# First loads of a decoder trunk: finer pieces of x, the norm vectors in x's rows, one weight buffer kept aside at the start

## The chip, the core and the metric

The kernel runs on one core of a Trainium2 chip. The metric is the device time of one execution in microseconds (us). TensorE (PE in the rows, PEld for its weight loads), VectorE (DVE), ScalarE (ACT), GpSimd (POOL) and SyncE (SP) run their own instruction streams and wait for each other by semaphores. Transfers between device memory and the on-chip memory are issued by SP (SPq in the rows), ACT (ACTq) or POOL, and run on the core's 16 DMA engines.

## What is computed

One decoder layer over 256 tokens of width 2048, all in float32: a token mixer with three groups of attention heads, a cross attention over 256 memory vectors, and a gated feed-forward block of width 5632, each with a residual add.

```
h = rms_norm(x, g_mix)
qa, ka, va, qb, kb, vb, qc, kc, vc = split(h @ w_in)
x = x + concat(diff_attention, moba_attention, dilated_attention) @ w_out
x = x + memory_cross_attention(rms_norm(x, g_cross), rms_norm(mem, g_mem), w_cq, w_ckv, w_co)
x = x + conv_glu_ffn(rms_norm(x, g_ffn), w_up, conv_w, conv_b, w_down)
out = rms_norm(x, g_final)
```

Each weight is read once.

## The kernel before

**Pieces and halves.** All weights are cut into pieces of 1 MB (128 partitions of 2048 floats), in the order in which they are used. A piece has two halves of 512 KB. Below, p0, p1, ... are the pieces and half 0, half 1, ... the halves, so half i is part i % 2 of piece i // 2. Each half goes through the same steps: it is loaded into a raw buffer; ACT copies it, rounded, into a tile `hi` (L141); DVE subtracts `hi` from it into a tile `lo` (L148); then PE multiplies (L296 with `hi`, L303 with `lo`). In the first chunk of `w_in` a half is 8 products with `hi` and 8 with `lo`. A raw buffer is free again once the `lo` tiles of both its halves are made.

**Buffers.** There are `NRAW = 4` raw buffers and `NSPLIT = 5` pairs of `hi` and `lo`. A piece's load waits until a raw buffer is free; a piece takes the buffer that the program frees first. `load` (L116) issues a whole piece from SP as one transfer, `load_half` (L130) half of one, `load_block` (L926) a quarter.

**x.** The input x lies transposed as 16 blocks of 128 channels by 256 tokens (`xT`, 2 MB in all). `high` (L194, on ACT) and `low` (L197, on DVE) multiply a block by its norm gain, a column of the tile `gT`, and write two parts of it into `hT`, which PE reads. Half i (for i up to 7) needs blocks 2i and 2i + 1. `put_x` does two blocks.

**Order.** There is no scheduler: each engine runs its instructions in the order in which this program writes them. The main loop (L1015) goes over the halves. In step i the `hi` copy and the `lo` subtraction of half i + `LEAD` (4 ahead) are written before half i's products; functions put down with `before(i, ...)` stand ahead of the `lo` of that step and those with `after(i, ...)` behind the products. Halves 2 to 7 are split by `after(i, ...)` of steps 0 to 5 instead, together with `put_x` (L973). Thus half 8 is split at the head of step 4, ahead of half 6, which is split at its end. At the head of step 4 the loads of p4, p5 and p6 are written on SP as well, p7 in step 6. The sums of squares of x (`square_part`, L215) and the norm factors (`norm_factors`, L230) are put down for steps 5 to 13: `fold` on DVE in step 10 and two small products on PE (`total`, L242) behind half 10.

**Loads.** SP issues its loads in order. Loads issued by SP and ACT take eight counters in turn (DMAHW0 to DMAHW7 in the rows below), so a load also waits until the load eight places earlier, which used its counter, has landed. The first loads stand at L933 to L944; p3 follows at L971. The norm gains, the first counter's load, are issued by ACT at L171 as an array of their own.

Of the kernel before, what the change touches and what calls it, by code (L numbers as in the profile page):

```python
# [11 lines left out]
F32 = mybir.dt.float32  # L12
# [5 lines left out]
P = 128  # L18
D = 2048
S = 256  # L20
NT = 2
KD = D // P
# [12 lines left out]
HALF = 1024  # L35
NRAW = 4
NSPLIT = 5
LEAD = 4
NACC = 5
MIX, MEM, CROSS, FFN = range(4)  # L40


BUCKET_AT = list(range(17)) + [22, 30, 40, 54, 73, 99, 134, 182, 246]
# [15 lines left out]


@with_exitstack
def trunk(ctx, tc, x, mem, gains, w_in, w_out, diff_lambda, rel_bias_table, w_cq, w_ckv, w_co, w_up, conv, w_down,
          g_final, onehot, biasadd, out):
    nc = tc.nc
    PE, DVE, ACT, POOL, SP = nc.tensor, nc.vector, nc.scalar, nc.gpsimd, nc.sync
    PSUM = bass.MemoryType.PSUM

    cst = ctx.enter_context(tc.tile_pool(name="cst", bufs=1))
    wpool = ctx.enter_context(tc.tile_pool(name="wpool", bufs=1))
# [23 lines left out]
    def small(n, name, bufs=4):  # L93
        return tmp.tile([P, n], F32, tag=f"sm_{name}", name=name, bufs=bufs)
# [10 lines left out]
    pieces = []  # L105
# [6 lines left out]
    def new_raw(p):  # L112
        if p.raw is None:
            p.raw = wpool.tile([P, 2 * HALF], F32, tag="raw", name="raw", bufs=NRAW)
# [15 lines left out]
    def load_half(p, h):  # L130
        new_raw(p)
        src = p.srcs[0]
        k = src.ap[1][1] // 2
        half = bass.AP(tensor=src.tensor, offset=src.offset + h * k * src.ap[1][0],
                       ap=[list(src.ap[0]), [src.ap[1][0], k], list(src.ap[2])])
        SP.dma_start(p.raw[:, h * HALF:(h + 1) * HALF].rearrange("p (k n) -> p k n", k=k), half)
# [20 lines left out]
    def before(i, f):  # L157
        pre.setdefault(i, []).append(f)
# [8 lines left out]

    gT = cst.tile([P, 4 * KD + 1], F32, name="gT")  # L170
    ACT.dma_start(gT, gains)  # L171
    subg = gT[:, 4 * KD:]
    mhalf = cst.tile([P, 1], F32, name="mhalf")
    POOL.memset(mhalf, -0.5)
    ones = cst.tile([P, 1], F32, name="ones")
    POOL.memset(ones, 1.0)
    ident = cst.tile([P, P], F32, name="ident")
    make_identity(nc, ident)
    ACT.copy(small(1, "first", 1), mhalf)


    xT = cst.tile([P, KD, S], F32, name="xT")


    def rstd_of(ss, n, width, r=None):
# [724 lines left out]
    for k in range(KF):  # L910
        src = bass.AP(tensor=w_down.tensor, offset=w_down.offset + k * P * D, ap=[[D, P], [1, D]])
# [9 lines left out]


    def load_x(a, n):
        SP.dma_start(xT[:, a:a + n, :], x[:, a:a + n, :])

    def load_block(p, k):  # L926
        new_raw(p)
        src = p.srcs[0]
        SP.dma_start(p.raw[:, k * 512:(k + 1) * 512],
                     bass.AP(tensor=src.tensor, offset=src.offset + k * src.ap[1][0],  # L930
                             ap=[list(src.ap[0]), list(src.ap[2])]))

    load_x(0, 2)  # L933
    load_block(pieces[0], 0)
    load_block(pieces[0], 1)
    load_x(2, 2)
    load_half(pieces[0], 1)
    load_x(4, 4)
    load_half(pieces[1], 0)
    load_half(pieces[1], 1)  # L940
    load_x(8, 4)
    load_half(pieces[2], 0)
    load_half(pieces[2], 1)
    load_x(12, 4)  # L944


    warm = acc_tile()
# [15 lines left out]
    p = pieces[0]  # L963
    p.parts[0] = hi, lo = [wpool.tile([P, HALF], F32R, tag=t, name=t, bufs=NSPLIT) for t in ("hi", "lo")]
    for j in range(2):
        c = slice(j * 512, (j + 1) * 512)
# [69 lines left out]
def packed(a):  # L1036

    return a.reshape(-1, P, a.shape[-1]).transpose(1, 0, 2)
# [24 lines left out]
```

## Time and profile before

| | |
|---|---|
| median of 3 runs | 1261.15 us (1261.11 to 1261.88) |
| profiled execution, its own time | 1260.96 us |
| its span, first to last instruction | 1259.2 us |
| PE busy | 1243.1 us (99%) |
| PE weight loads busy | 1078.2 us (86%) |
| DVE busy | 831.4 us (66%) |
| ACT busy | 630.3 us (50%) |
| bytes moved | 233.23 MB, mean 185 GB/s |

The profiled execution took 1.8 us more than its span. Busy time is an average over the whole span; the change touches the first loads, so the table says little of it, and the stretches at the start have to be read one by one.

### The profile page before, as it was taken

Reading aid. Unit: us, or ns where it says so; the run is one execution under the profiler, and the core shown is the slowest. Engines: PE = TensorE matmul, PEld = TensorE weight load, DVE = VectorE, ACT = ScalarE, POOL = GpSimd, SP = SyncE. Lnnn points to the kernel's source line nnn. Section 1 sums busy time; section 2 is a strip of 40 time slices with the busy share of each in tenths; the row PEclk is TensorE's granted clock in tenths of the full one; section 3 lists DMA queues with packets and bytes.
Section 4 is the critical chain, followed back from the end, with each engine's and each line's share of the span. In section 5 each row is a group of like instructions: output and inputs, shape, how many; then the busy total and the mean of one; then the engine's idle time right before and its main releaser. Section 6 shows DMA issues by size and latency. Waiting matters only on the chain.

```text
span 1259.2 us, 17608 instructions
## 1 busy us (share of the span) xinstructions
PE 1243.1 (99%) x6928; PEld 1078.2 (86%) x6928; DVE 831.4 (66%) x1350; ACT 630.3 (50%) x979; POOL 12.2 (1%) x22
## 2 busy tenths in 40 slices
PE   7999999999999999999999999999999999999997
PEld 6888888988888899888888888888888888888885
DVE  5755677566568877776667768767676754544555
ACT  6545555556455656545444444444444544444444
POOL 0000000000000000000000000000000000000000
PEclk9999999999999999999999999999999999999999
DMA  8755554554566544565565565555656555555541
GB/s 301 236 176 188 186 167 162 181 183 159 174 223 215 170 167 162 202 203 171 167 200 182 186 197 174 183 199 184 198 170 201 186 183 200 181 187 200 175 160 67
DMA packets 104835, 233.23 MB, mean 185 GB/s; under 512 B 4336, under 2 KB 14896, under 8 KB 98992
## 3 DMA queue, kind: packets, MB, share of 16 engines
q1 hardware_dynamic: 104576, 232.05, 55.2%
q8 instruction: 54, 0.88, 0.3%
q14 instruction: 29, 0.24, 0.1%
q10 hardware_dynamic: 144, 0.03, 0.0%
q0 software_dynamic: 32, 0.02, 0.0%
HBM read 229.97 MB, written 2.12 MB: 184 GB/s over the span
## 4 chain that ended last, share of the span: by engine, by line
issue 58%; PE 39%; DMA 2%; DVE 0%; POOL 0%; ACT 0%; SPq 0%; DVEq 0%; POOLq 0%; ACTq 0%
PE acc L296 16%; PE acc L303 9%; PE acc L342 3%; PE acc L344 3%; PE acc L343 3%; DMA raw<-in_w_in 2%; PE at L402 1%; PE acc L299 1%; PE acc L298 1%; PE at L421 0%; PE at L445 0%; PE at L473 0%; PE at L474 0%; ACT hi L141 0%; POOL raw L866 0%
## 5 line engine op out<-in xcount | busy, mean ns | idle before, releaser
L148 DVE TENSOR_TENSOR lo<-raw,hi 128x1024 fp32r<-128x1024 f32 x423 | 517.1, 1223 | 368.1 <-ACT hi L141 367.5
L141 ACT CAST hi<-raw 128x1024 fp32r<-128x1024 f32 x423 | 442.9, 1048 | 480.6 <-PE acc L296 281.0
L296 PE MATMUL acc<-hT,hi 128*128 128x512 f32 x1776 | 631.3, 396 | 4.7 <-ACT hi L141 4.7
L303 PE MATMUL acc<-hT,lo 128*128 128x256 f32 x1840 | 517.7, 283 | 0.9 <-DVE lo L148 0.9
L296 PEld LDWEIGHTS acc<-hT,hi 128*128 128x128 f32 x1776 | 334.0, 188 | 82.0 <-ACT hi L141 5.3
L303 PEld LDWEIGHTS acc<-hT,lo 128*128 128x128 f32 x1840 | 345.6, 188 | 1.6 <-DVE lo L148 1.3
L296 PE MATMUL at<-hT,hi 128*128 128x512 f32 x528 | 189.6, 394 | 0.0
L303 PE MATMUL at<-hT,lo 128*128 128x256 f32 x528 | 149.3, 283 | 0.0
L296 PEld LDWEIGHTS at<-hT,hi 128*128 128x128 f32 x528 | 99.2, 188 | 22.8
L303 PEld LDWEIGHTS at<-hT,lo 128*128 128x128 f32 x528 | 99.3, 188 | 0.0
L854 PE MATMUL acc<-hi,al 128*128 128x512 f32 x220 | 86.8, 395 | 0.0
L853 PE MATMUL acc<-lo,ah 128*128 128x512 f32 x220 | 86.8, 395 | 0.0
L852 PE MATMUL acc<-hi,ah 128*128 128x512 f32 x220 | 86.8, 395 | 0.0
L342 PE MATMUL acc<-hi,hT 128*128 128x256 f32 (+1 forms) x224 | 74.8, 334 | 0.0
L344 PE MATMUL acc<-hi,hT 128*128 128x256 f32 (+1 forms) x224 | 74.0, 330 | 0.0
L343 PE MATMUL acc<-lo,hT 128*128 128x256 f32 (+1 forms) x224 | 73.9, 330 | 0.0
L852 PE MATMUL at<-hi,ah 128*128 128x512 f32 x132 | 52.1, 395 | 0.0
L854 PE MATMUL at<-hi,al 128*128 128x512 f32 x132 | 52.1, 395 | 0.0
L853 PE MATMUL at<-lo,ah 128*128 128x512 f32 x132 | 52.1, 394 | 0.0
L789 ACT ACTIVATE y<-y 128x256 f32<-128x256 f32 x44 | 18.4, 419 | 66.4 <-DVE y L785 66.4
L852 PEld LDWEIGHTS acc<-hi,ah 128*128 128x128 f32 x220 | 41.5, 188 | 9.7
L853 PEld LDWEIGHTS acc<-lo,ah 128*128 128x128 f32 x220 | 41.5, 188 | 9.7
(157 smaller groups left out, 1004.2 us busy)
## 6 DMA issues: line engine op xcount, KB each, us to landing
raw<-in_w_up SPq DMA_DIRECT2D x88, 1024.0 KB, 5.1
raw<-in_w_in SPq DMA_DIRECT2D x45, 1024.0 KB, 5.3
raw<-in_w_down SPq DMA_DIRECT2D x44, 1024.0 KB, 4.9
raw<-in_w_out SPq DMA_DIRECT2D x12, 1024.0 KB, 5.3
raw<-in_w_ckv SPq DMA_DIRECT2D x8, 1024.0 KB, 5.6
raw<-in_w_out SPq DMA_DIRECT2D x8, 512.0 KB, 5.0
raw<-in_w_cq SPq DMA_DIRECT2D x4, 1024.0 KB, 5.4
raw<-in_w_co SPq DMA_DIRECT2D x4, 1024.0 KB, 5.3
```

What stands on the lines that cost most here:

```text
L141: ACT.copy(hi, p.raw[:, h * HALF:(h + 1) * HALF])
L148: DVE.tensor_tensor(lo, p.raw[:, h * HALF:(h + 1) * HALF], hi.bitcast(F32), op=ALU.subtract)
L296: PE.matmul(accs[n], w, x, start=(i == 0), stop=False)
L298: PE.matmul(accs[n][:, :S], w, x[:, :S], start=(i == 0), stop=False)
L303: PE.matmul(accs[n][:, :S], lo[:, j, n * P:(n + 1) * P], src()[:, korder[i], :S], start=False, stop=(i == len(korder) - 1))
L342: PE.matmul(o, xh, hi[:, j, :], start=(i == 0), stop=False)
L343: PE.matmul(o, xh, lo[:, j, :], start=False, stop=False)
L344: PE.matmul(o, xl, hi[:, j, :], start=False, stop=(i == len(korder) - 1))
L789: after(cur[0] + 1 + n, lambda: ACT.activation(gate[k], gate[k], AF.Silu))
L852: PE.matmul(o, ah, wh, start=(k == 0), stop=False)
L853: PE.matmul(o, ah, wl, start=False, stop=False)
L854: PE.matmul(o, al, wh, start=False, stop=(k == KF - 1))
```

## The change

Four edits, all at the start of the program.

- The norm gains are no array of their own. They stand in the first 65 of 128 columns that are put ahead of x's columns, so that x and the gains are one tile `xin`, and the first load of x brings the gains too: 640 columns of 4 bytes on each of 128 partitions in place of 512, 320 KB in place of 256 KB.
- ACT's first instruction is now the load of the first quarter of p0 (block 0), in the place where the gains' load stood. SP no longer issues it.
- x's blocks 4 to 7 come as two loads of 256 KB, with the first half of p1 between them, in place of one of 512 KB.
- After p0, p1 and p2 have taken three raw buffers, the fourth is taken by a tile `hold`. POOL sets one column of it and DVE reads that column in step 8, which frees it. p3 is written behind that.

```diff
+GCOLS = 128
-    gT = cst.tile([P, 4 * KD + 1], F32, name="gT")
-    ACT.dma_start(gT, gains)
+    xin = cst.tile([P, GCOLS + KD * S], F32, name="xin")
+    gT = xin[:, :4 * KD + 1]
     subg = gT[:, 4 * KD:]
+    xT = xin[:, GCOLS:].rearrange("p (k n) -> p k n", k=KD)
...
-    ACT.copy(small(1, "first", 1), mhalf)
-    xT = cst.tile([P, KD, S], F32, name="xT")
...
     def load_x(a, n):
-        SP.dma_start(xT[:, a:a + n, :], x[:, a:a + n, :])
+        c = slice(GCOLS + a * S if a else 0, GCOLS + (a + n) * S)
+        SP.dma_start(xin[:, c], x[:, c])
-    def load_block(p, k):
+    def load_block(eng, p, k):
...
     load_x(0, 2)
-    load_block(pieces[0], 0)
-    load_block(pieces[0], 1)
+    load_block(ACT, pieces[0], 0)
+    load_block(SP, pieces[0], 1)
+    ACT.copy(small(1, "first", 1), mhalf)
     load_x(2, 2)
     load_half(pieces[0], 1)
-    load_x(4, 4)
+    load_x(4, 2)
     load_half(pieces[1], 0)
+    load_x(6, 2)
     load_half(pieces[1], 1)
     load_x(8, 4)
     load_half(pieces[2], 0)
     load_half(pieces[2], 1)
     load_x(12, 4)
+    hold = wpool.tile([P, 2 * HALF], F32, tag="raw", name="raw", bufs=NRAW)
+    POOL.memset(hold[:, :1], 0.0)
+    before(8, lambda: DVE.tensor_copy(small(1, "held", 1), hold[:, :1]))
```

**The first loads on SP.** Before, from the start of the program (`raw_98` is p0's buffer, `raw_104` p1's; 128x512 is a quarter of a piece or two blocks of x, 128x2x512 a half of a piece):

```order
L924 DMA xT_93<-in_x 128x512
L929 DMA raw_98<-in_w_in 128x512 x2
L924 DMA xT_93<-in_x 128x512
L136 DMA raw_98<-in_w_in 128x2x512
L924 DMA xT_93<-in_x 128x1024
L136 DMA raw_104<-in_w_in 128x2x512
L136 DMA raw_104<-in_w_in 128x2x512 [waits DMAHW0_49]
```

After, at the same place (`raw_94` is p0, `raw_102` p1):

```order
L924 DMA xin_80<-in_x 128x640
L929 DMA raw_94<-in_w_in 128x512
L924 DMA xin_80<-in_x 128x512
L137 DMA raw_94<-in_w_in 128x2x512
L924 DMA xin_80<-in_x 128x512
L137 DMA raw_102<-in_w_in 128x2x512
L924 DMA xin_80<-in_x 128x512
L137 DMA raw_102<-in_w_in 128x2x512 [waits DMAHW0_49]
```

One quarter of p0 has left SP, so each load up to p0's second half stands one place earlier; x's blocks 4 to 7 are two rows.

**The loads of whole pieces on SP.** Before, from x's last four blocks on (`raw_156` is p3, then p4, p5, p6 and, `raw_328`, p7; the counters of p3 to p7 are DMAHW5, 6, 7, 0 and 1 before and after):

```order
L924 DMA xT_93<-in_x 128x1024 [waits DMAHW4_49]
L126 DMA raw_156<-in_w_in 128x4x512 [waits DMAHW5_49]
L126 DMA raw_264<-in_w_in 128x4x512 [waits DMAHW6_49,DVE_49]
L126 DMA raw_266<-in_w_in 128x4x512 [waits DMAHW7_49,DMAHW0_49,DVE_49]
L126 DMA raw_268<-in_w_in 128x4x512 [waits DMAHW3_49,DMAHW2_49,DVE_49]
L126 DMA raw_328<-in_w_in 128x4x512 [waits DMAHW6_49,DMAHW1_49,DVE_49]
```

After (`raw_157` is p3, `raw_265` p4, `raw_267` p5, `raw_269` p6, `raw_329` p7, `raw_397` p8, `raw_449` p9; five small loads stand between p7 and p8):

```order
L924 DMA xin_80<-in_x 128x1024 [waits DMAHW4_49]
L127 DMA raw_157<-in_w_in 128x4x512 [waits DMAHW5_49,DVE_49]
L127 DMA raw_265<-in_w_in 128x4x512 [waits DMAHW6_49,DMAHW0_49,DVE_49]
L127 DMA raw_267<-in_w_in 128x4x512 [waits DMAHW3_49,DMAHW7_49,DMAHW2_49,DVE_49]
L127 DMA raw_269<-in_w_in 128x4x512 [waits DMAHW6_49,DVE_49]
...
L127 DMA raw_397<-in_w_in 128x4x512 [waits DMAHW7_49,DVE_49]
L127 DMA raw_449<-in_w_in 128x4x512 [waits DMAHW0_49,DVE_49]
```

The wait for DVE has come to p3 as well, and each piece takes over the buffer that p4, p5, ... took one place earlier: p3 takes p0's, p4 p1's, p5 p2's. p6 now waits for counter 6, p4's, that is, it takes p4's buffer, which p7 had before. The buffer of `hold` goes to p9.

**ACT around the splits of halves 5 to 6.** Before (128x1024 are `hi` copies; `raw_108` is p2, half 5; `raw_264` p4, half 8; `raw_156` p3, half 6):

```order
L141 CAST hi_260<-raw_108 128x1024 [waits DMAHW3_49,DVE_49,PE_49]
L141 CAST hi_270<-raw_264 128x1024 [waits DMAHW6_49,DVE_49,PE_49]
L195 ACTIVATE hT_137<-xT_93,gT_80 128x256 [waits DMAHW4_49]
L195 ACTIVATE hT_137<-xT_93,gT_80 128x256
L141 CAST hi_294<-raw_156 128x1024 [waits DMAHW5_49,DVE_49,PE_49]
```

After:

```order
L142 CAST hi_261<-raw_107 128x1024 [waits DMAHW3_49,DVE_49,PE_49]
L142 CAST hi_271<-raw_265 128x1024 [waits DMAHW6_49,DVE_49,PE_49]
L194 ACTIVATE hT_138<-xin_80 128x256 [waits DMAHW4_49]
L194 ACTIVATE hT_138<-xin_80 128x256
L142 CAST hi_295<-raw_157 128x1024 [waits DMAHW5_49,DVE_49,PE_49]
```

Nothing moved here: in both, half 8's copy, which waits for p4's load (counter 6), stands ahead of half 6's.

## Rows read from the trace of the kernel before

**Rows 1.** Windows by stretch: us; busy per engine (instructions); PEclk, DMA share, GB/s.

```profile
0.00:45.00 45.00, 37.91 (x204) 32.94 (x205) 30.12 (x41) 28.68 (x43) 0.74 (x8) 0.96 0.84 294
45.00:1250.00 1205.00, 1204.98 (x6726) 1045.25 (x6725) 798.22 (x1302) 598.92 (x932) 10.93 (x13) 1.00 0.54 181
```

**Rows 2.** Timeline of PE: start us, duration us, what, [idle before, releaser].

```profile
10.11 2.12 PE L296 MATMUL acc<-hT,hi 128*128 128x512 f32 x8 [1.17 <-ACT hi L141]
...
28.00 0.50 PE L296 MATMUL acc<-hT,hi 128*128 128x512 f32 x1 [3.56 <-ACT hi L141]
29.44 0.58 PE L303 MATMUL acc<-hT,lo 128*128 128x256 f32 x1 [0.94 <-DVE lo L148]
29.82 0.63 PE L296 MATMUL acc<-hT,hi 128*128 128x512 f32 x1
...
32.34 0.40 PE L296 MATMUL acc<-hT,hi 128*128 128x512 f32 x1
...
32.70 0.40 PE L296 MATMUL acc<-hT,hi 128*128 128x512 f32 x1
...
44.64 0.50 PE L242 MATMUL at<-ones,sq 128*128 128x1 f32 x4
```

**Rows 3.** Timeline of ACT, the same columns.

```profile
4.39 0.91 ACT L195 ACTIVATE hT<-xT,gT 128x256 fp32r<-128x256 f32 x2 [1.75 <-DMA gT<-in_gains]
...
25.16 1.04 ACT L141 CAST hi<-raw 128x1024 fp32r<-128x1024 f32 x1 [6.68 <-DMA raw<-in_w_in]
...
37.64 1.04 ACT L141 CAST hi<-raw 128x1024 fp32r<-128x1024 f32 x1
```

**Rows 4.** Chain of work that ended last, first 50 us: start us, us, what.

```profile
2.58 6.42 DMA raw<-in_w_in
...
11.35 13.71 DMA raw<-in_w_in
```

**Rows 5.** Timeline of SP: issues of the first loads, of p3, p5, p6, p7.

```profile
0.73 0.38 SPq L924 DMA_DIRECT2D xT<-in_x  x1
1.17 0.89 SPq L929 DMA_DIRECT2D raw<-in_w_in  x2
...
9.01 0.37 SPq L126 DMA_DIRECT2D raw<-in_w_in  x1
...
15.96 0.37 SPq L126 DMA_DIRECT2D raw<-in_w_in  x1
...
19.94 0.37 SPq L126 DMA_DIRECT2D raw<-in_w_in  x1
...
30.55 0.37 SPq L126 DMA_DIRECT2D raw<-in_w_in  x1
```

**Rows 6.** Issue to landing, us, for p3, p5, p6, p7 in turn.

```profile
raw<-in_w_in SPq DMA_DIRECT2D x1, 1024.0 KB, 13.3
...
raw<-in_w_in SPq DMA_DIRECT2D x1, 1024.0 KB, 11.8
...
raw<-in_w_in SPq DMA_DIRECT2D x1, 1024.0 KB, 10.5
...
raw<-in_w_in SPq DMA_DIRECT2D x1, 1024.0 KB, 5.5
```

**Rows 7.** Windows of the first loads, columns as in the first group.

```profile
5.50:7.00 1.50, 1.50 (x10) 1.19 (x9) 1.48 (x3) 1.30 (x4) 0.00 (x0) 1.00 0.81 244
9.00:27.00 18.00, 14.32 (x80) 12.27 (x80) 9.88 (x14) 10.21 (x17) 0.00 (x0) 1.00 1.04 392
29.00:29.50 0.50, 0.06 (x1) 0.06 (x1) 0.50 (x2) 0.50 (x2) 0.00 (x0) 0.50 0.07 25
```

**Rows 8.** Timeline of DVE.

```profile
28.17 2.35 DVE L148 TENSOR_TENSOR lo<-raw,hi 128x1024 fp32r<-128x1024 f32 x2
...
31.23 2.57 DVE L148 TENSOR_TENSOR lo<-raw,hi 128x1024 fp32r<-128x1024 f32 x2
...
42.40 1.15 DVE L237 TENSOR_TENSOR sq<-sq 128x512 f32<-128x512 f32 x2
```

More of the change, by code (lines that the diff above doesn't have):

```diff
@@ L61, in trunk @@
 @with_exitstack
-def trunk(ctx, tc, x, mem, gains, w_in, w_out, diff_lambda, rel_bias_table, w_cq, w_ckv, w_co, w_up, conv, w_down,
+def trunk(ctx, tc, x, mem, w_in, w_out, diff_lambda, rel_bias_table, w_cq, w_ckv, w_co, w_up, conv, w_down,
           g_final, onehot, biasadd, out):
@@ L923, in load_x @@
     def load_x(a, n):
-        SP.dma_start(xT[:, a:a + n, :], x[:, a:a + n, :])
-    def load_block(p, k):
+        c = slice(GCOLS + a * S if a else 0, GCOLS + (a + n) * S)
+        SP.dma_start(xin[:, c], x[:, c])
+    def load_block(eng, p, k):
         new_raw(p)
         src = p.srcs[0]
-        SP.dma_start(p.raw[:, k * 512:(k + 1) * 512],
-                     bass.AP(tensor=src.tensor, offset=src.offset + k * src.ap[1][0],
-                             ap=[list(src.ap[0]), list(src.ap[2])]))
+        eng.dma_start(p.raw[:, k * 512:(k + 1) * 512],
+                      bass.AP(tensor=src.tensor, offset=src.offset + k * src.ap[1][0],
+                              ap=[list(src.ap[0]), list(src.ap[2])]))
     load_x(0, 2)
-    load_block(pieces[0], 0)
-    load_block(pieces[0], 1)
+    load_block(ACT, pieces[0], 0)
+    load_block(SP, pieces[0], 1)
+    ACT.copy(small(1, "first", 1), mhalf)
     load_x(2, 2)
     load_half(pieces[0], 1)
-    load_x(4, 4)
+    load_x(4, 2)
     load_half(pieces[1], 0)
+    load_x(6, 2)
     load_half(pieces[1], 1)
@@ L1045 @@
     v = {name: np.asarray(a) for name, a in inputs.items()}
-    gains = np.concatenate([packed(v[n][0][:, None])[:, :, 0] for n in ("g_mix", "g_mem", "g_cross", "g_ffn")]
-                           + [v["diff_subln"][0][:, None]], axis=1)
+    gains = [packed(v[n][0][:, None])[:, :, 0] for n in ("g_mix", "g_mem", "g_cross", "g_ffn")]
+    x = np.zeros((P, GCOLS + KD * S), np.float32)
+    x[:, :4 * KD + 1] = np.concatenate(gains + [v["diff_subln"][0][:, None]], axis=1)
+    x[:, GCOLS:] = packed(v["x"][0].T).reshape(P, -1)
     conv = packed(np.concatenate([v["conv_w"][0], v["conv_b"]], axis=0).T)
     onehot, add = bias_constants()
-    arrays = {"x": packed(v["x"][0].T), "mem": packed(v["mem"][0].T), "gains": gains, "w_in": v["w_in"][0],
+    arrays = {"x": x, "mem": packed(v["mem"][0].T), "w_in": v["w_in"][0],
               "w_out": v["w_out"][0], "diff_lambda": v["diff_lambda"][0], "rel_bias_table": v["rel_bias_table"],
```

## The prediction

> **What bounds the kernel now.** I read the windows first. From 45 us on PE is busy for 1204.98 of 1205.00 us: nothing that starts a load earlier or later can give anything there, unless it makes PE wait anew. In the first 45 us PE is busy for 37.91, so all that there is to win lies there, some 7 us, of which the first matmuls need a part in any case [rows 1].
>
> The timeline of PE says where. Half 1 starts at 10.11 after 1.17 us of waiting. Halves 1 to 5 then follow without a wait. Half 6 is the large one: 3.56 us idle before 28.00, one product, and 0.94 us more before 29.44 [rows 2]. Right behind it a product with `hi` and one with `lo` take 2.52 / 4 = 0.63 us together (29.82 to 32.34, four pairs), and 0.36 us from 32.34 on; the granted clock reads 0.50 in that stretch [rows 2, 7], the lower of the two levels, 1.2 GHz, after PE had stood idle for those 3.56 and 0.94 us. That costs 4 x (0.63 - 0.36) = 1.1 us more. After that no wait is left.
>
> Half 6's wait ends with ACT, and the timeline of ACT shows that ACT itself had waited: its copy at 25.16 came after 6.68 us of waiting for a load [rows 3]. That copy is half 8's, not half 6's; it stands ahead in ACT's order, and it needs p4. From it to PE there are a copy, two blocks of x, and half 6's copy: 28.00 - 25.16 = 2.84 us. So **p4's landing sets the start of half 6**, and with it the end of the kernel. The chain says the same: it goes back over a load issued at 11.35, 13.71 us long, which is p4, and before that over one issued at 2.58, 6.42 us long, p0's second half, on which half 1 waits [rows 4].
>
> What sets p4's landing? Issue plus time to landing gives, for p3, p4, p5 and p6: 9.01 + 13.3 = 22.3, 11.35 + 13.71 = 25.1, 15.96 + 11.8 = 27.8, 19.94 + 10.5 = 30.4 [rows 4 to 6]. They are issued 2.3 to 4.6 us apart but land 2.7 to 2.8 us apart, which is 1.05 MB at the 392 GB/s that the DMA engines move between 9 and 27 us [rows 7]. The loads pass one behind the other, in the order of issue, and the engines are full. p4 lands when everything ahead of it has passed: 2 MB of x and five pieces. **Its own issue time has some 10 us to spare.**
>
> **The change part by part.**
>
> *The buffer kept aside.* p3, p4, p5 and p6 each take a buffer that is freed later, at the times at which before the next piece was issued: p3 at 11.35 instead of 9.01, p4 at 15.96 instead of 11.35, p5 at 19.94 instead of 15.96, p6 at 30.55 instead of 19.94 [rows 4, 5]. For p3 to p5 this costs nothing as long as the work ahead in the queue covers it. An idle queue lands 1 MB in 5.5 us [rows 6], so p4 could land at 21.5 at the earliest, and p5 at 25.4; the queue makes them land at 25.1 and 27.8 anyway. It also gains nothing: what stands behind p4 does not hold it up.
> p6 is the one that could hurt. Issued at 30.55 into an empty queue it lands at about 36.05. Its first user, ACT's copy of half 12, began at 37.64 [rows 3], so 1.6 us are spare. A later p6 would delay the DVE work on the norm behind it, which ended at 42.40 + 1.15 = 43.55, while PE came to it at 44.64 [rows 2, 8]: 1.1 us more. PE waits only if p6 lands 2.7 us later than that, past 38.7. Price: nothing. p7 now waits for half 7's `lo`, the first of the two subtractions at 31.23 [rows 8], so about 32.5, and the five small loads queue behind it; half 14 is two halves behind half 12. p8 and p9 (behind DVE's new read in step 8) are for halves 16 and 18. From p10 on the buffers come free as before. POOL's memset and DVE's one-column copy fall where neither sets PE's pace.
>
> *The gains in x's rows.* The first load grows by 64 KB, the gains' own 32.5 KB are gone: 33 KB more, at 392 GB/s 0.08 us later for all that follows. ACT's first operation waited for the gains until 4.39 [rows 3]; now it waits for the larger first load, alone. I cannot read its landing from this trace; half 0 may start a few tenths earlier or later. It has cover: half 1 cannot start before p0's second half, and the 1.17 us of idle time ahead of half 1 is what it would eat up.
>
> *x's blocks 4 to 7 in two loads.* The same bytes in one more load. Half 2 could start earlier, but runs right behind half 1 in any case: nothing.
>
> *Block 0 from ACT's queue.* SP issues one load every 0.44 us (0.73 to 1.17) [rows 5], so all of SP's later first loads are issued 0.44 us earlier. Is the stream short of loads there? From 5.5 to 7.0 us the engines move 244 GB/s instead of 392, at a busy share of 0.81 [rows 7], a shortfall of (392 - 244) x 1.5 = 222 KB, or 0.57 us of the full rate. They starve there although loads were issued long before, so a second queue that delivers beside SP's can fill some of it. I take 0.44 us for the issue and a bit under half of the shortfall, 0.25. The ends are: nothing of either, or all of both.
>
> The Trainium skill, page "DMA: Bandwidth & Descriptors", section "Issuing engines are not separate DMA queues", speaks against the second term: loads from several engines run on the same DMA engines and interleave, and a second issuer saves only the time to issue. By that the sum would be -0.44 + 0.08 = -0.36 us.
>
> **Sum:** -0.44 - 0.25 + 0.08 = -0.61 us for p0's second half and, since the queue is full from then on, for p4 too. Halves 1 and 6 both start 0.6 us earlier, PE's idle time ahead of half 6 stays about 3.5 us, and the slow stretch of the clock stays. Ends: +0.08 and -0.44 - 0.57 + 0.08 = -0.93. Against the profiled execution's own 1260.96 us that is 1260.35; the median of the runs is 0.19 higher, so I say 1260.5.
>
> **The rivals.**
> - *Nothing comes of it* (chance 0.13): block 0, now beside the larger first piece of x, only takes its bandwidth, and the stream is as late as before: 1261.2.
> - *The lagging DMA engine* (0.14). A load has landed when the last of the 16 engines is through with its share. Between 29.0 and 29.5 us 25 GB/s are moved at a share of 0.07 [rows 7], that is, one engine of 16 alone was still at work on p6, a good 2 us after the bulk had ended at about 27. So p4's landing is also that of one late engine. Nothing in the change addresses it, but with other first pieces on two queues another engine may be less late. If p4 then lands 1.6 us earlier on top, the idle time before half 6 falls to about 2 us, the clock stays up as it does after the 1.17 us before half 1 (1.00 from 9 to 27 us [rows 7]), and 0.6 + 1.6 + 1.1 = 3.3 us are won: 1257.8.
> - *The hold works as a shield* (0.06): p4 no longer shares the engines with p5 and p6. For that they would have to share; landings in order of issue, 2.7 us apart, say they do not. If they do after all, p4 lands perhaps 1.4 us earlier, half of one piece's time, and the clock stays: 0.6 + 1.4 + 1.1 = 3.1 us, 1258.0.
> - *Slower: p6 comes too late* (0.05). If p6 in truth waits for DVE's read of `hold` in step 8, it is issued at about 37.6 and lands at 43.1 instead of the 37.64 at which half 12's copy began: 5.5 us later, of which 1.1 are spare. PE waits 4.4 us at the norm's products behind half 10 and loses 1.1 us to the clock: 1261.15 - 0.6 + 5.5 = 1266.1. Against it: in the order p6 waits for counter 6, so it takes p4's buffer, and that is free at 30.55. It decides from a landing past 38.7 on.
>
> **How the numbers follow.** The forecast has a chance of 0.60, its own range is 1260.1 to 1261.4; 0.02 is left for something slower that I do not see. 0.2%, 2.5 us, is about what a measurement of this kernel can tell from no change. Faster by more than that are the lagging engine and the shield, 0.20; slower the late p6 and the rest, 0.07, which I round to 0.06; the same 0.74. A range of 1257.7 to 1261.8 takes in both faster cases and the case in which nothing comes of it.
>
> **What would show it.** In the profile after: half 1's start at about 9.5 with little idle time before it; ACT's long wait, in front of half 8's copy, ending at about 24.4; PE idle 3 to 4 us before half 6 and the lower clock after it; p3 to p5 landing 2.7 us apart still; p6 issued at about 30 and landed by 36; no wait of PE at the products of L242. I am wrong if half 6's wait shrinks by more than a microsecond, if the lower clock vanishes, if the loads cease to land one behind the other, or if PE waits anywhere after half 6.

## The result and the profile after

The changed kernel takes 1252.17 us, the median of six runs (1251.78 to 1252.86), against 1261.38 us of six runs of the kernel before on the same chip (1261.11 to 1261.88): a ratio of 0.9932 [0.9921, 0.9942]. It is **faster by 9.2 us**, where 0.9 us were forecast against that median; the range, down to 1257.7, misses it. The profiled execution took 1252.27 us, 1250.5 of them span (before: 1260.96 and 1259.2).

The first 45 us do not hold 9 us. Windows of the kernel after, first the two stretches of [rows 1] (the second only up to 1240 us), then two of the first loads:

```profile
0.00:45.00 45.00, 39.40 (x209) 34.18 (x210) 30.52 (x44) 29.50 (x43) 1.20 (x10) 0.92 0.85 298
45.00:1240.00 1195.00, 1194.98 (x6716) 1037.39 (x6716) 796.29 (x1300) 596.66 (x928) 10.36 (x13) 1.00 0.55 182
5.50:7.00 1.50, 1.29 (x8) 0.93 (x7) 1.48 (x4) 1.50 (x5) 0.00 (x0) 1.00 1.01 376
28.00:30.00 2.00, 1.86 (x6) 1.67 (x7) 2.00 (x5) 2.00 (x3) 0.00 (x0) 0.50 0.00 0
```

PE is busy all the time from 45 us on, as before, and yet about 10 us fewer pass until the same work is done. Two more views say where. First the lines of PE that mark the way: the small products of the norms (first and last start), and the first of the three lines of products in the last stage. Each row ends with the start of its first and of its last instruction. Before:

```profile
L242 PE MATMUL at<-ones,sq x16: 165/250/250, 44.6 to 517.4; 128*128 128x1 f32 x16
...
L852 PE MATMUL acc<-hi,ah x220: 390/393/405, 1004.6 to 1249.3; 128*128 128x512 f32 x110
```

After:

```profile
L241 PE MATMUL at<-ones,sq x16: 166/250/250, 43.8 to 513.6; 128*128 128x1 f32 x16
...
L851 PE MATMUL acc<-hi,ah x220: 392/399/399, 994.9 to 1240.5; 128*128 128x512 f32 x110
```

At 44 us the kernel after is 0.8 us ahead, at 515 us 3.8, at 1000 us 9.7, and at the end 8.8. So 0.8 us come from the start, **8.9 us arise in stretches in which PE never waits**, and 0.9 are given back in the last stage.

Second, the two windows in which only one kind of product runs: `w_up` at 800 to 900 us, and the last stage at 1040 to 1200. Before:

```profile
800.00:900.00 100.00, 100.00 (x571) 87.64 (x571) 72.85 (x113) 47.02 (x66) 0.00 (x0) 1.00 0.55 182
1040.00:1200.00 160.00, 160.00 (x690) 129.77 (x689) 80.17 (x87) 68.38 (x85) 0.00 (x0) 1.00 0.55 189
```

After:

```profile
800.00:900.00 100.00, 100.00 (x579) 88.07 (x578) 73.68 (x111) 46.37 (x63) 0.00 (x0) 1.00 0.56 185
1040.00:1200.00 160.00, 160.00 (x688) 128.70 (x687) 79.55 (x86) 69.01 (x87) 0.00 (x0) 1.00 0.54 190
```

At the same granted clock of 1.00, PE gets through 579 matmuls in 100 us instead of 571. A pair of a `hi` and a `lo` product takes 200 / 579 = 0.345 us instead of 200 / 571 = 0.350. That is 5 ns, good to about 1 ns, as a count is good to one product; some 2300 pairs (1776 + 528 `hi` products) at 4 ns make the 9 us. In the last stage it is 688 instead of 690. The same instructions run at another pace.

The start itself went much as forecast. Timeline of PE after:

```profile
6.21 2.14 PE L295 MATMUL acc<-hT,hi 128*128 128x512 f32 x8 [0.21 <-DVE hT L197]
...
9.15 2.14 PE L295 MATMUL acc<-hT,hi 128*128 128x512 f32 x8
...
26.70 0.79 PE L295 MATMUL acc<-hT,hi 128*128 128x512 f32 x1 [3.34 <-ACT hi L142]
28.14 0.58 PE L302 MATMUL acc<-hT,lo 128*128 128x256 f32 x1 [0.65 <-DVE lo L149]
28.51 0.63 PE L295 MATMUL acc<-hT,hi 128*128 128x512 f32 x1
...
32.35 0.40 PE L295 MATMUL acc<-hT,hi 128*128 128x512 f32 x1
...
43.80 0.50 PE L241 MATMUL at<-ones,sq 128*128 128x1 f32 x4
```

Timeline of ACT after:

```profile
8.05 1.05 ACT L142 CAST hi<-raw 128x1024 fp32r<-128x1024 f32 x1 [0.56 <-DMA raw<-in_w_in]
...
23.85 1.05 ACT L142 CAST hi<-raw 128x1024 fp32r<-128x1024 f32 x1 [6.29 <-DMA raw<-in_w_in]
...
36.92 1.03 ACT L142 CAST hi<-raw 128x1024 fp32r<-128x1024 f32 x1
```

Half 1 starts 0.96 us earlier and without a wait; half 8's copy, which waits for p4, 1.3 us earlier; half 6 still has its wait of 3.34 us, the lower clock (0.50 from 28 to 30 us) and its pace of some 0.63 us for a pair behind it. That pace now lasts for six pairs (28.51 to 32.35) where it lasted for four, and the two more give back 2 x (0.64 - 0.36), some 0.5 us of the 1.3. No engine waits for p6: half 12's copy at 36.92 has no idle time before it.

**Where the pace can come from.** The same product reads the same shapes, but the tiles lie elsewhere. Merging the gains into x's rows lengthens what lies ahead of the weight buffers by 224 B a partition (65 columns, 260 B rounded up to 288, become 128 columns, 512 B). `held`, the new one-column tile, lies between the weight buffers and `hT` and takes 32 B. So `hT` and the last stage's operands `ah`, `al` moved by 32 B against `hi` and `lo`. In `w_up` PE loads `hi` and `lo` as weights and streams `hT` past them; in the last stage it loads `ah` and `al` and streams `hi` and `lo`. Where the built programs put the first buffer of each (bytes from the partition's start; e8, s1 and s2 have those of the kernel after):

```
             hi      lo      hT      ah     hT-hi   hT-lo   ah-hi   against before
before    67296   87776  117600  209760    50304   29824  142464
after     67520   88000  117856  210016    50336   29856  142496   +32 all
e1        67520   88000  117856  210016    50336   29856  142496   +32 all
e2        67552   88032  117920  210080    50368   29888  142528   +64 all
e3        67328   87808  117632  209792    50304   29824  142464   0 (all four tiles +32)
e4        67296   87776  117632  209792    50336   29856  142496   +32 all
e5        67296   87776  117696  209856    50400   29920  142560   +96 all
e6        67296   87776  117728  209888    50432   29952  142592   +128 all
e7        67520   88000  117856  210048    50336   29856  142528   +32, ah +64
e9        67296   87808  117632  209792    50336   29824  142496   hi +32, lo 0
e10       67520   88000  117856  210112    50336   29856  142592   +32, ah +128
```

### The profile page after: what moved, and what is told of

Read it like the earlier page. It is cut to its first block, busy times and chain, and to the rows that moved or that the text cites. A ratio compares the mean times of both kernels' runs of the same rounds, so it can differ in the third digit from the quotient of the medians.

```text
span 1250.5 us, 17611 instructions
## 1 busy us (share of the span) xinstructions
PE 1235.8 (99%) x6928; PEld 1072.4 (86%) x6928; DVE 830.8 (66%) x1351; ACT 630.0 (50%) x979; POOL 12.3 (1%) x23
## 4 chain that ended last, share of the span: by engine, by line
issue 58%; PE 37%; DMA 2%; DVE 2%; ACT 0%; POOL 0%; DVEq 0%; POOLq 0%; SPq 0%; ACTq 0%
PE acc L295 16%; PE acc L302 8%; PE acc L341 3%; PE acc L343 3%; PE acc L342 3%; DMA raw<-in_w_in 1%; PE at L401 1%; DMA xin<-in_x 1%; DVE lo L149 1%; PE at L420 0%; PE at L444 0%; DVE hT L197 0%; PE acc L298 0%; PE acc L297 0%; PE at L472 0%
## 5 line engine op out<-in xcount | busy, mean ns | idle before, releaser
L302 PE MATMUL acc<-hT,lo 128*128 128x256 f32 x1840 | 512.0, 280 | 0.6 <-DVE lo L149 0.6
L853 PEld LDWEIGHTS acc<-hi,al 128*128 128x128 f32 x220 | 41.3, 188 | 10.8
```

Of the source, the lines that this page charges most:

```text
L302: PE.matmul(accs[n][:, :S], lo[:, j, n * P:(n + 1) * P], src()[:, korder[i], :S], start=False, stop=(i == len(korder) - 1))
L853: PE.matmul(o, al, wh, start=False, stop=(k == KF - 1))
```

## The experiments

Theory A: tile addresses set a product's time. Its forms in the expectations differ in what counts: the address itself, or (A2 and what follows from it, with different periods) the distance between the two operands of a product. Theory B, the rival: the new loads do it, by what they move or when. Ratios are to the kernel before on the same chip.

**e1: the kernel before, with the tiles where the kernel after has them.** Two tiles that nothing uses; loads and instructions as before.

```diff
     ss3 = small(8, "ss3", 1)
+    tmp.tile([P, 8], F32, name="padt")
...
     convT = cst.tile([P, KF, CW + 1], F32, name="convT")
+    cst.tile([P, 56], F32, name="padc")
```

> The kernel before with nothing changed but two unused tiles, 224 bytes behind the constants and 32 bytes behind the small temporaries: raw, hi, lo, hT and all that lies behind them stand at the very addresses that they have in the changed kernel, while every load is that of before. Theory A (addresses: the products run quicker because the tiles hi and lo begin at a multiple of 64 bytes instead of 32 past one): some 7.9 us are won, the part of the gain that comes after 45 us, so about 1253.4, and a pair of products takes 346.7 ns instead of 351.1. Theory B (loads: which piece takes which raw buffer, and when it is loaded, goes on after the start and makes PE quicker): 1261.4, as before.

1252.7 us, 0.9937 [0.9922, 0.9952]. Nearly the whole gain, with not one load changed. B falls as the cause of the 8 us. The windows of e1 have the counts of the kernel after, 579 and 688:

```profile
800.00:900.00 100.00, 100.00 (x579) 88.04 (x578) 73.66 (x111) 46.37 (x63) 0.00 (x0) 1.00 0.54 186
1040.00:1200.00 160.00, 160.00 (x688) 128.69 (x687) 79.58 (x86) 69.01 (x87) 0.00 (x0) 1.00 0.55 190
```

**e2: the kernel after, with `padc` and `padt` of 32 B each**: the new loads at a distance of +64.

```diff
     ss3 = small(8, "ss3", 1)
+    tmp.tile([P, 8], F32, name="padt")
...
     convT = cst.tile([P, KF, CW + 1], F32, name="convT")
+    cst.tile([P, 8], F32, name="padc")
```

> The changed kernel with two unused tiles of 32 bytes, so that hi and lo begin again 32 bytes past a multiple of 64, and hT too, as before the change. Theory A: only the gain at the start is left, 0.8 us at 45 us, so about 1260.5. Theory B: 1252.2, as the changed kernel.

1258.95 us, 0.9985 [0.9976, 0.9995]: within 0.2% of before. With all of the change's loads in place, 64 unused bytes take most of the gain away. `w_up` is slower than before (568 matmuls instead of 571), the last stage quicker (701 instead of 690):

```profile
800.00:900.00 100.00, 100.00 (x568) 86.85 (x567) 71.66 (x111) 46.65 (x66) 0.00 (x0) 1.00 0.54 184
1040.00:1200.00 160.00, 160.00 (x701) 131.28 (x700) 80.82 (x87) 70.61 (x88) 0.00 (x0) 1.00 0.54 191
```

**e3 and e4: address or distance.** e3 is before with only `padc`, 32 B: all these tiles move together. e4 is before with only `padt`, 32 B: `hi` and `lo` stay, `hT`, `ah` and `al` move.

```diff
     convT = cst.tile([P, KF, CW + 1], F32, name="convT")
+    cst.tile([P, 8], F32, name="padc")
```

> The kernel before with one unused tile of 32 bytes behind the constants: raw, hi and lo begin at multiples of 64 bytes, and so do hT and the parts of a in the last product. Theory A in its plain form (an address at a multiple of 64 is quicker for each operand): at least as quick as with hi and lo alone, 1253.4 or less. Theory A2 (what matters is whether the two operands of a product begin alike or 32 bytes apart): 1261.4, since before both began 32 past. Theory B: 1261.4.

```diff
     ss3 = small(8, "ss3", 1)
+    tmp.tile([P, 8], F32, name="padt")
```

> The kernel before with one unused tile of 32 bytes behind the small temporaries: hi and lo stay 32 bytes past a multiple of 64, hT and the parts of a begin at multiples of 64. Theory A, plain: a gain only as far as the streamed operand's address counts, between 0 and 8 us. Theory A2 (alike or apart): about 1253.4, as with hi and lo alone. Theory B: 1261.4.

e3 takes 1260.17 us, 0.9997 [0.9988, 1.0006], e4 1253.27, 0.9941 [0.9926, 0.9955]. Moving all four tiles by 32 B does nothing that can be seen; moving `hT`, `ah` and `al` alone by 32 B gives what e1 gave. The form of A that looked at the address alone falls. The windows of e3 are those of before to one product:

```profile
800.00:900.00 100.00, 100.00 (x572) 87.63 (x571) 73.53 (x115) 46.23 (x65) 0.00 (x0) 1.00 0.53 180
1040.00:1200.00 160.00, 160.00 (x690) 129.71 (x689) 79.44 (x86) 69.09 (x86) 0.00 (x0) 1.00 0.55 188
```

**e5 and e6: larger distances**, before with `padt` of 96 and of 128 B (`[P, 24]` and `[P, 32]` in e4's line).

> The kernel before with an unused tile of 96 bytes behind the small temporaries: hT and the parts of a stand 96 bytes further from hi and lo than before. The runs so far: with 0 more a pair of products in the w_up stage takes 351.5 ns, with 32 more 347.1, with 64 more 353.7. Theory A3 (the distance counts, with a period of 128 bytes, and 32 less is as good as 32 more): about 1253. Rival A2 (only alike or 32 apart within 64 bytes): also about 1253. Rival A4 (the distance counts, but over a longer period): anything between 1250 and 1264. Theory B (loads): 1260.5, as before.

> The same with 128 bytes. Theory A3 (period of 128 bytes): the products take what they took before, 351.5 ns for a pair, 1260.5 us. Rival A2: the same. Rival A4 (longer period): a pair takes something else.

e5: 1265.22 us, 1.003 [1.0018, 1.0041], slower than before. e6: 1248.83 us, 0.99 [0.9886, 0.9915], quicker than the kernel after. So +96 does not act like +32, nor +128 like 0: if there is a period, it is not 32, 64 or 128 B. e6 has 579 matmuls in `w_up`, like the kernel after, and 708 in the last stage; first e5, then e6:

```profile
800.00:900.00 100.00, 100.00 (x568) 86.84 (x567) 71.53 (x110) 45.93 (x64) 0.00 (x0) 1.00 0.55 189
1040.00:1200.00 160.00, 160.00 (x688) 128.50 (x686) 79.61 (x86) 68.59 (x87) 0.00 (x0) 1.00 0.54 185
...
800.00:900.00 100.00, 100.00 (x579) 87.48 (x578) 74.25 (x115) 46.71 (x64) 0.00 (x0) 1.00 0.55 187
1040.00:1200.00 160.00, 160.00 (x708) 132.53 (x707) 81.81 (x88) 70.76 (x88) 0.00 (x0) 1.00 0.56 191
```

**e7 and e10: only the last stage's operands moved**, the kernel after with an unused tile behind `a`: 32 B in e7, 96 B in e10 (`[P, 24]`), which puts `ah` and `al` at +64 and at +128, where e2 and e6 had their good last stages. **e8** is the kernel after once more, on e7's chip.

```diff
         ffn["a"] = f.tile([P, KF, S], F32, name="a")
+        f.tile([P, 8], F32, name="padf")
```

> The changed kernel with an unused tile of 32 bytes behind the activations of the feed-forward block, so that the two parts of a, which the last product streams against, stand 64 bytes further from hi and lo than before the change, not 32, while hT stays at 32. In that stage the products took 232.4 ns at 0, 233.3 at 32 and 228.9 at 64. If the distance of the two operands of the product is all that counts, the stage's 968 or so products gain 4.4 ns each, 4.3 us: 1247.9. If what counts is where hi and lo themselves begin, nothing changes: 1252.2.

> The changed kernel with an unused tile of 96 bytes behind the activations of the feed-forward block: the parts of a stand 128 bytes further from hi and lo than before the change, hT 32 further as in the changed kernel. Where all stood 128 further the last products took 226.7 ns each, at 64 further 228.9. If only the distance between the two operands counts, 968 products gain 2.2 ns more, 2 us: 1245.5. If more than this distance counts, 1247.5 or above.

> The changed kernel once more, on the same chip as the others, for the part of the loads: with the addresses alone (old loads) the kernel took 1252.7, with addresses and new loads 1252.17 on another chip. If the new loads are worth the 0.6 us of the prediction, this run's median is some 0.6 under what the addresses alone give against the same before, and PE's first product behind half 10 stands 0.6 us or more ahead of that of kernels with old loads. If they are worth nothing, it is spread around theirs.

e7: 1247.51 us, 0.9891 [0.9876, 0.9905]. e10: 1244.78 us, 0.9872 [0.9857, 0.9887]. e8: 1252.57 us, 0.9932 [0.9917, 0.9947]. A distance chosen for the last stage acts on that stage alone, by the count that it had elsewhere: e7 has 578 and 701 matmuls in the two windows, where the kernel after has 579 and 688. The stage has 3 x 352 = 1056 products, not the 968 of the expectations; the 4.4 and 6.6 ns that these give for each make 4.6 and 7.0 us, and 5.1 (against e8) and 7.5 (against s1 and s2, on e10's chip) were measured. e10, with `w_up` as in the kernel after and the last stage as in e6, is **the quickest kernel here, 16 us under the kernel before**:

```profile
800.00:900.00 100.00, 100.00 (x579) 87.99 (x578) 73.58 (x113) 46.36 (x63) 0.00 (x0) 1.00 0.55 184
1040.00:1200.00 160.00, 160.00 (x708) 132.53 (x707) 82.32 (x89) 70.80 (x90) 0.00 (x0) 1.00 0.55 195
```

**e9: `hi` and `lo` moved apart.** Before, with 32 B between the `hi` and the `lo` buffers, so that `hT` is at +32 from `hi` and at 0 from `lo`.

```diff
-    p.parts[0] = hi, lo = [wpool.tile([P, HALF], F32R, tag=t, name=t, bufs=NSPLIT) for t in ("hi", "lo")]
+    hi = wpool.tile([P, HALF], F32R, tag="hi", name="hi", bufs=NSPLIT)
+    wpool.tile([P, 8], F32, name="padw")
+    lo = wpool.tile([P, HALF], F32R, tag="lo", name="lo", bufs=NSPLIT)
+    p.parts[0] = hi, lo
```

> The kernel before with one unused tile of 32 bytes between hi and lo: hT stands 32 bytes further from hi than before, and as far from lo as before. In the w_up stage it is, from the start of one product to the start of the next, 231.0 ns for hi's and 120.5 for lo's where both stand as before, and 229.6 and 117.5 where both stand 32 further. Theory O (a product is slowed by the place of its own weights): hi's 229.6, lo's 120.5, a pair 350.1, about 1259. Theory V (a product is slowed by the weights that are loaded for the next one while it streams): hi's 231.0, since lo's weights are loaded beside it, and lo's 117.5; a pair 348.5, about 1256. In the last product, which loads ah and al and streams hi and lo, both parts stand 32 further from hi than before and as before from lo.

1262.68 us, 1.0014 [1.0005, 1.0023], with 571 and 687 matmuls in the two windows: nothing of the gain, and neither theory of this run is met.

```profile
800.00:900.00 100.00, 100.00 (x571) 87.37 (x570) 72.68 (x113) 47.14 (x66) 0.00 (x0) 1.00 0.53 182
1040.00:1200.00 160.00, 160.00 (x687) 128.47 (x686) 79.93 (x87) 68.42 (x85) 0.00 (x0) 1.00 0.55 190
```

Between 800 and 900 us it is, in the mean, 233.3 ns from the start of a `hi` product to the next start, and 117.8 for a `lo` product. The second number is V's (117.5) and not O's (120.5): `lo`'s products run as at +32 though `lo` itself stands at 0, so the place of their own weights does not by itself set their pace. The first is slower than either theory said. By the table e9 differs from e4 in nothing but the place of `lo`, and that took all of e4's gain away. The distance between `hi` and `lo` changes here too. Which of the reads act on each other stays open.

**s1: the kernel after without the hold.** p3 to p6 are issued as before; the tile `held` and its copy stay, so that the addresses do too.

```diff
-    hold = wpool.tile([P, 2 * HALF], F32, tag="raw", name="raw", bufs=NRAW)
-    POOL.memset(hold[:, :1], 0.0)
-    before(8, lambda: DVE.tensor_copy(small(1, "held", 1), hold[:, :1]))
+    before(8, lambda: DVE.tensor_copy(small(1, "held", 1), mhalf))
```

> The changed kernel without the buffer kept aside: p3 to p6 are issued as before the change, all tiles stay where the changed kernel has them (DVE's one-column copy is left in, from another tile). If the loads pass one behind the other, the hold is worth nothing: 1252.2, p4 lands about 16 us after p0's second half, as it does with the hold. If it works as a shield for p4, PE starts half 6 some 1.4 us later than in the changed kernel and the time is 1253.5 to 1255.

**s2: the kernel after with block 0 issued by SP.**

```diff
-    load_block(ACT, pieces[0], 0)
+    load_block(SP, pieces[0], 0)
```

> The changed kernel with block 0 issued by SP again. If the earlier issue is what moves the start, half 1 starts 0.4 to 0.7 us later than in the changed kernel, at 9.9 to 10.2, and half 6 as much later: 1252.8. If the start is moved by the gains in x's rows or the finer parts, half 1 starts at about 9.2 to 9.7 and the time is 1252.2.

s1: 1252.19 us, 0.9929 [0.9914, 0.9944]. s2: 1252.31 us, 0.9933 [0.9916, 0.9949]. Both are the kernel after: neither the hold nor ACT's queue is worth anything that can be seen. The intervals are some 4 us wide, so a few tenths of a us would not show in these times. Half 6 starts as there, too. Timeline of PE, s1:

```profile
26.60 0.49 PE L295 MATMUL acc<-hT,hi 128*128 128x512 f32 x1 [2.68 <-ACT hi L142]
28.04 0.58 PE L302 MATMUL acc<-hT,lo 128*128 128x256 f32 x1 [0.94 <-DVE lo L149]
```

And s2:

```profile
26.66 0.49 PE L295 MATMUL acc<-hT,hi 128*128 128x512 f32 x1 [2.85 <-ACT hi L142]
28.10 0.58 PE L302 MATMUL acc<-hT,lo 128*128 128x256 f32 x1 [0.95 <-DVE lo L149]
```

## Why the prediction was wrong

**The step that failed** stands at the head of the prediction: PE is busy from 45 us on, so "nothing that starts a load earlier or later can give anything there". As a sentence on loads it holds. But the sum took from it that the whole change can give nothing there, and so counted 1205 us of products as a constant. The change also moved tiles, and the 32 B by which it changed the distance between a product's operands were worth 7 to 8 us (e1 and e4: 7.8 and 7.2 us under before with the old loads). No term, rival or condition named it, though the diff showed two places where the layout changes. That PE is busy says that it does not wait; it does not say that the work has a fixed duration.

**The sum for the start** was -0.61 us. With the old loads and the new distance, e1 and e4 take 1252.7 and 1253.27 us; with the new loads and the same distance, the kernel after, e8, s1 and s2 take 1252.17, 1252.57, 1252.19 and 1252.31. The means are 0.7 us apart, those of the ratios (0.9939 and 0.9932) 0.9 us; the intervals of these ratios overlap, so the times alone do not show it. The traces do: the first `lo` product of half 6 starts at 28.88 us in the mean of the seven traces with the old loads, and at 27.95 in that of the seven with the new ones, 0.9 us earlier. Single traces with the old loads spread from 27.68 (e3) to 29.69 (e5), so the size is good to about half a us only, and that the one pair of profiles has 1.3 us at this place is in part luck.

**Its parts** are borne out less than their sum. The rate from 5.5 to 7 us did rise, from 244 to 376 GB/s (246 to 283 in the other traces with the old loads, 324 to 365 in those with the new ones). But I gave 0.44 us to block 0's move to ACT's queue and 0.25 to the second queue beside SP's. s2 takes both back, and no loss can be seen: the rate in that window is 356 GB/s, and its copy for half 8 stands at 23.82 us, that of the kernel after at 23.85 and that of e8, the same kernel, at 23.49. With a spread like that a loss of 0.3 us is not excluded; the 0.69 us of both terms are not borne out. What is left are the other edits of the first loads, the gains within x's rows and the smaller parts of x; no run took these apart, so that the gain comes from them is not shown. The Trainium skill, page "DMA: Bandwidth & Descriptors", section "Issuing engines are not separate DMA queues", speaks against the second term, since by it a second issuer saves only the time to issue. s2 agrees as far as one trace can tell: without the second issuer no loss is seen.

**The hold at nothing** was right (s1). Its late p6 harmed nothing: in the kernel after it is issued at 29.25 us, the engines move 0 GB/s from 28 to 30 us, it lands at 34.56, and no copy or product waits for it. p3, p4 and p5 land at 21.04, 23.75 and 26.38 us, 2.6 to 2.7 us apart as forecast. That it works as a shield for p4 falls: in s1, without it, half 8's copy begins at 23.76 us.

**Half 6's wait and the lower clock stay**, as forecast: 3.34 us idle instead of 3.56, 0.50 behind it. The rival of the lagging engine did not come true in the kernel after; in the other traces with the new loads the wait is 2.4 to 2.9 us (e2, e7, e8, e10, s1, s2), and the clock falls all the same. It took for granted that the clock stays up when the wait is only about 2 us; in e3, where the wait is 1.92 us and one of 0.80 follows, the granted clock is 0.50 from 28 to 30 us as well.

**Half 1** was forecast at about 9.5 us with little idle time; it starts at 9.15 with none. That single trace flatters: in the seven with the new loads half 1 starts at 9.60 us in the mean (9.15 to 10.01), in the seven with the old ones at 10.11 (9.92 to 10.28).

## What to carry to other kernels

Where an engine is busy throughout, ask of a change not only whether it takes waits away but whether it alters what the busy instructions cost, the place of their operands included: a new one-column tile was enough. Compare the number of instructions in the same long window of both traces before looking for a cause in the part that was edited. And before crediting an edit that adds, drops or merges tiles, run the old kernel with unused tiles that put its operands at the new addresses; if the gain is there too, the distance can be tuned by itself, as e7 and e10 did for the last stage.

## What of the hardware was not expected

The pace of TensorE's products of `fp32r` tiles (float32, rounded, as `hi` and `lo` hold it) depends on how far apart their operands lie in SBUF, the on-chip memory, at a granted clock of 1.00 and with no wait. In 100 us of `w_up` 571 products are done at the distance of before, 579 at +32 B, 568 at +64 and +96 and 579 at +128; in 160 us of the last stage 690, 688, 701, 688 and 708. That is 2% and 3% between the best and the worst. Moving all operands together by 32 B does nothing (e3: 572 and 690). What else moves data then does not make it. Once the last `lo` tile is made, no load and no splitting of weights runs beside the last stage's products. Windows of these 11 us, before and e10:

```profile
1238.70:1249.70 11.00, 11.00 (x49) 8.94 (x48) 8.71 (x16) 5.30 (x14) 2.21 (x2) 1.00 0.00 0
...
1223.70:1234.70 11.00, 11.00 (x50) 9.01 (x48) 8.64 (x17) 5.40 (x14) 2.15 (x2) 1.00 0.00 0
```

The DMA engines move nothing, and yet from start to start the products take 232.4 ns there in the kernel before, 233.3 in the kernel after, 228.9 in e7 and 226.7 in e10, each as in its stage as a whole. For `w_up` there is no such stretch to look at. This would fit reads of the two operands, or of the weights loaded for the next product, that get in each other's way; that is only argued, and e9 did not settle between which reads. Whether the pattern repeats beyond 128 B was not tried.
